# HGRN2: the gated output goes into the tile of the intra-chunk weights, and the sums of output weights are spread over other heads

## The chip, the cores and the metric

One core of a Trainium2 chip runs the whole program: a two-layer backbone (layer 0: neighbourhood attention and mLSTM; layer 1: HGRN2) over 1024 latent tokens and 256 context tokens of width 1024, all in float32. The metric is the device time of one execution in microseconds; the kernel before is given by the median of three.

## The reference

Both parts of the change lie in layer 1, the HGRN2 mixer. Cut to what matters:

```python
def _gla_chunkwise(q, k, v, lf, S):          # per head, both directions
    def step(S, xs):
        b = jnp.cumsum(lfc, axis=2)
        o = einsum('bhtk,bhkv->bhtv', qc * exp(b), S)
        pair = exp(where(tri, b[:, :, :, None, :] - b[:, :, None, :, :], -inf))
        a = einsum('bhtk,bhtsk->bhts', qc, pair * kc[:, :, None, :, :])
        o = o + einsum('bhts,bhsv->bhtv', a, vc)
        S = exp(bL[:, :, 0])[..., None] * S + einsum('bhsk,bhsv->bhkv', kc * exp(bL - b), vc)
        return S, o

def merge(o, z):
    o = _rms(o, h_norm)                      # over the 128 columns of a head
    return (o * silu(z)) @ w_out             # 16 heads x 128 columns -> 1024
```

`a` are the intra-chunk weights, `o` a head's output, `z` its gate.

## The kernel before

The 16 heads of layer 1 run one after the other in the loop of `build` (L1348 on). The recurrence is worked in 8 chunks of 128 tokens. For a head h:

- `hg_intra` (L976) makes K and Q, the diagonal product in strips of 64x64 (L1006, on `gq`, masked into `gD` at L996) and then seven levels (`hg_level`, L1025): strips of K and Q on PE (L1006, on `gksel` and `gQ`), products on DVE that carry the decay one level on (L1051, L1055), a masked copy into D (L1057). New Q comes from four products (L987). After the last level ACT copies the intra-chunk weights into the tile A (`gA`, one buffer, 128 x 8 x 128; L1061, L1062).
- `hg_vz` (L921) projects v and z: a group of 24 matmuls for v of the context (copied by ACT into the tile `gEc` at L930), then four groups of 48 matmuls of 256 columns, a pair of token tiles each ("projection matmuls", `mm<-wzh` and `mm<-wzl`, L128 to L130). From each group's PSUM bank ACT copies v (L940) and a sigmoid (L942), and DVE writes z (L943, tile `gz`, one buffer). The tag `mm` has two PSUM banks.
- `hg_close` transposes K into `gkn`; `hg_ctx` (L947) makes the context's state in the tiles `gEc`, `gq` and `gknc` (sums at L969).
- `hg_scan` (L1064) runs the states backward (L1071) and the output forward: per chunk L1082 (A times v), L1083 and L1084 (Q times the states), and L1087 for the next state. Four chunks share the one PSUM bank `acc`. After the 4th and the 8th chunk: four squares with sums on ACT (L1098), two steps of the inverse root on POOL (L154, L156), o times z on DVE (L1102), and the scaling on POOL (L1103).
- `hg_proj(h + 1)` projects the next head's decays and q (weights `wh`, `wl`).
- `hg_out` (L1135) transposes the scaled product, four chunks at a time, on PE (L1140), ACT scales it into `gyt` (L1142) and POOL's queue writes it to DRAM (L1143, `yd2`).
- `wo_sums` (L1110) prepares the output stage, which multiplies sums of blocks of the output weights: one call takes a 128 x 256 piece of each of four blocks. On POOL's queue: four loads (L1116) into `gknc` and `gEc`, four subtractions (L1117), four stores (L1123). Sixteen calls are needed; heads 0 to 7 have one each, heads 8 to 11 two.
- `y_diff` (L1126) behind heads 1 to 8 makes a difference of two halves of an earlier head's y, in the same two tiles on the same queue (L1129 to L1132).

The order of the instructions on each engine is fixed when the program is built: a planner puts them in order by priority (the strips and level products are marked urgent) and by its own notion of when each could start. So work of head h + 1 (its levels and its projection of v and z) runs between the scan and the transposes of head h; I call that stretch the seam of head h + 1, and it opens with that head's diagonal strips. `gknc` and `gEc` have one buffer each and serve `hg_vz`, `hg_ctx`, `wo_sums` and `y_diff` in turn.

Behind the loop the output stage (L1363 on) multiplies y by the prepared blocks. Its first products are planned into the last head. Its later tiles (`gbc`, `woraw`, `oys`) take over memory of the head loop's pools, and their loads are issued from SP's queue (L1399 on).

Of the kernel before, what the change touches and what calls it, by code (L numbers as in the profile page):

```python
# [13 lines left out]
ALU = mybir.AluOpType  # L14
# [4 lines left out]
P = 128  # L19
# [25 lines left out]
class Prog:  # L45
# [1018 lines left out]
    def hg_scan(self, st, H, S, pool):  # L1064
        nc = self.nc
        v, z = st["v"], st["z"]
        Sf, Sb = S
        sb = {7: Sb}
        for c in range(7, 0, -1):
            u = self.ps("s", [P, P])  # L1070
            nc.tensor.matmul(u, lhsT=H["kn"][c // 4][1][:, c % 4, :], rhs=v[:, c, :], start=True, stop=True)  # L1071
            s = self.t(pool, [P, P], F32, "gS1", 10)
            nc.vector.scalar_tensor_tensor(
                out=s, in0=sb[c], scalar=H["T"][:, 1, c : c + 1], in1=u, op0=ALU.mult, op1=ALU.add
            )
            sb[c - 1] = s
        for c in range(8):
            cs = slice(c * P, (c + 1) * P)
            if c % 4 == 0:
                o4 = self.ps("acc", [P, 4, P])  # L1080
            o = o4[:, c % 4, :]
            nc.tensor.matmul(o, lhsT=H["A"][:, c, :], rhs=v[:, c, :], start=True, stop=False)  # L1082
            nc.tensor.matmul(o, lhsT=H["Q"][:, 0, cs], rhs=sb[c], start=False, stop=False)  # L1083
            nc.tensor.matmul(o, lhsT=H["Q"][:, 1, cs], rhs=Sf, start=False, stop=True)  # L1084
            if c < 7:
                u = self.ps("s", [P, P])
                nc.tensor.matmul(u, lhsT=H["kn"][c // 4][0][:, c % 4, :], rhs=v[:, c, :], start=True, stop=True)  # L1087
                s = self.t(pool, [P, P], F32, "gS0", 2)
                nc.vector.scalar_tensor_tensor(
                    out=s, in0=Sf, scalar=H["T"][:, 0, c : c + 1], in1=u, op0=ALU.mult, op1=ALU.add  # L1090
                )
                Sf = s
            if c % 4 < 3:
                continue
            ss = self.t(pool, [P, 4], F32, "gss", 2)
            jk = self.t(pool, [P, P], F32, "gjk", 1)
            for i in range(4):
                nc.scalar.activation(jk, o4[:, i, :], AF.Square, accum_out=ss[:, i : i + 1])  # L1098
            self.rsqrt(ss, ss, 1.0 / P)

            z4 = z[:, c - 3 : c + 1, :]
            nc.vector.tensor_tensor(out=z4, in0=o4, in1=z4, op=ALU.mult)  # L1102
            nc.gpsimd.tensor_tensor(out=z4, in0=z4, in1=ss.unsqueeze(2).to_broadcast([P, 4, P]), op=ALU.mult)  # L1103

    def quarters(self, pool):
        two = [self.t(pool, [P, 2 * SQ], F32, t, 1) for t in ("gknc", "gEc")]
# [39 lines left out]
    def build(self):  # L1146
        tc, nc, a = self.tc, self.nc, self.a
        dma = nc.sync.dma_start
        with ExitStack() as es:
# [22 lines left out]
            def load(name, shape, eng=nc.gpsimd):  # L1172
# [12 lines left out]
                out=self.qkn, in0=qkn[:, 0:1], scalar1=qkn[:, 1:2], scalar2=0.125, op0=ALU.mult, op1=ALU.mult  # L1185
# [14 lines left out]
            for i in range(2):  # L1200
# [6 lines left out]
                out=self.lb[:, 1, :], in0=self.lb[:, 0, :], scalar1=-1.0, scalar2=1.0, op0=ALU.mult, op1=ALU.add  # L1207
# [35 lines left out]
            with tc.tile_pool(name="na", bufs=2) as pool, self.pp.phase(tq=1, s=2, acc=1):  # L1243
                qk = self.na_qk(0, pool)
                z = self.na_z(0, pool)
                ahead = [("k", 0), ("q", 1), ("k", 1), ("q", 2), ("k", 2), ("q", 3)]
                for p2 in range(8):
                    self.na_attn(p2, qk, z, pool)
                    if p2 < 7:
# [5 lines left out]
                        z = self.na_z(p2 + 1, pool)  # L1255
# [5 lines left out]
            with tc.tile_pool(name="ml", bufs=2) as pool, self.pp.phase(s=2, acc=2):  # L1261
# [9 lines left out]
                st, parts = self.ml_load(0, pool)  # L1271
                for ld in parts:
                    ld()
                for h in range(4):
                    nxt, parts = self.ml_load(h + 1, pool) if h < 3 else (None, None)
                    self.ml_rec(h, st, pool, parts)
                    st = nxt
# [65 lines left out]
            with l1:  # L1343
                pool = l1.enter_context(tc.tile_pool(name="hg", bufs=2))
                self.rawp = pool
                l1.enter_context(self.pp.phase(s=3, acc=1))
                st = self.hg_proj(0, pool, wf)
                for h in range(16):  # L1348
                    hv = self.hg_intra(st, pool)
                    self.hg_vz(h, st, pool)  # L1350
                    self.hg_close(hv, pool)
                    S = self.hg_ctx(st, pool)
                    self.hg_scan(st, hv, S, pool)
                    z = st["z"]
                    if h < 15:
                        st = self.hg_proj(h + 1, pool)
                    self.hg_out(h, z, pool, self.yd2)
                    for i in ([h] if h < 8 else [2 * h - 8, 2 * h - 7] if h < 12 else []):
                        self.wo_sums(i // 2, i % 2, pool)
                    if 0 < h < 9:  # L1360
                        self.y_diff(h - 1, pool)

                rh.close()  # L1363
                yp = es.enter_context(tc.tile_pool(name="oy", bufs=1, side="right"))
                wo, wr, raw = [(yp, "wo", 8)], [(self.wp, "w", 4)], [yp, 4, "woraw"]
                assert self.slabs == 4
                S, W, y2 = self.sy, a["woc"], self.yd2
                acc = [self.t(yp, [P, 4, 512], F32, f"oacc{i}", 1) for i in range(2)]
                block = lambda src, ring, later=None, raw=raw: self.wblock(
                    None, "wo", [src], 8, 512, raw, later=later, ring=ring  # L1370
                )
                p, u = acc

                def add(out, x, y, eng=nc.vector):
                    eng.tensor_tensor(out=out, in0=x, in1=y, op=ALU.add)

                w = block(W[0:D, 0:512], wo * 8, None, [self.rawp, 3, "wraw"])
                self.out_part(w, 0, 0, y2, yp, lambda t, ps: nc.scalar.copy(acc[0][:, t, :], ps))
                w = block(self.sw[1], wr * 4 + wo * 4)
                self.out_part(w, 0, 0, S, yp, lambda t, ps: add(u[:, t, :], ps, p[:, t, :]))  # L1380
                w2 = block(W[D : 2 * D, 0:512], wo * 4 + wr * 4)

                yh, yl = [[], []], [[], []]
                for k in (0, 4):
                    for t in range(2):
                        for to, fr in zip((yh[t], yl[t]), self.out_y(t, 1, y2, yp, 4, ks=(k,))):
                            to += fr
# [225 lines left out]
```

## Time and profile before

| | us |
|---|---|
| median of 3 runs | 3467.52 (3466.03 to 3476.98) |
| the profiled execution, whole | 3470.15 |
| its span | 3468.4 |
| granted PE clock over the span | 0.992 |
| head loop, diagonal of head 0 to last transposes | 1891.5 to 3326.5 |
| behind it | 141.9 |

The profile's page gives busy time by engine: PE is TensorE's matmuls, PEld its weight loads, DVE is VectorE, ACT ScalarE, POOL GpSimd, SP the queue that issues most loads. In rows in order of time, the first column is the start within the span, the second the length in us; a bracket tells how long the engine stood idle before and what it waited for. Float32 matmuls take two passes each, so x32 strips are 16 matmuls. Steps between the starts of neighbouring matmuls tell the rate, not their lengths, since they overlap.

### The profile page before, as it was taken

Reading aid. Unit: us, or ns where it says so; the run is one execution under the profiler, and the core shown is the slowest. Engines: PE = TensorE matmul, PEld = TensorE weight load, DVE = VectorE, ACT = ScalarE, POOL = GpSimd, SP = SyncE. Lnnn points to the kernel's source line nnn. Section 1 sums busy time; section 2 is a strip of 40 time slices with the busy share of each in tenths; the row PEclk is TensorE's granted clock in tenths of the full one; section 3 lists DMA queues with packets and bytes.
Section 4 is the critical chain, followed back from the end, with each engine's and each line's share of the span. In section 5 each row is a group of like instructions: output and inputs, shape, how many; then the busy total and the mean of one; then the engine's idle time right before and its main releaser. Section 6 shows DMA issues by size and latency. Waiting matters only on the chain.

```text
span 3468.4 us, 64675 instructions
## 1 busy us (share of the span) xinstructions
PE 3386.4 (98%) x25100; PEld 2983.5 (86%) x25100; DVE 2089.2 (60%) x4824; ACT 1440.2 (42%) x3353; POOL 674.2 (19%) x1044
## 2 busy tenths in 40 slices
PE   8999999999999999999999999999999999999987
PEld 5779998889989888898878999888888899998876
DVE  4546665666655566687666555555555555555667
ACT  5445554554543444454354333333333333333432
POOL 2222221222211112221100111111111322000023
PEclk9999999999999999999999999999999999999998
DMA  5542222322223434444652111111111211110364
GB/s 205 174 133 59 78 77 77 90 80 72 81 88 96 150 115 128 132 130 144 211 168 79 50 56 56 59 59 58 56 59 57 69 62 62 44 38 26 122 204 145
DMA packets 331540, 333.59 MB, mean 96 GB/s; under 512 B 30985, under 2 KB 277961, under 8 KB 331233
## 3 DMA queue, kind: packets, MB, share of 16 engines
q1 hardware_dynamic: 291008, 222.76, 21.7%
q0 software_dynamic: 40224, 106.69, 9.1%
q8 instruction: 198, 3.24, 0.4%
q14 instruction: 110, 0.89, 0.1%
HBM read 259.40 MB, written 69.79 MB: 95 GB/s over the span
## 4 chain that ended last, share of the span: by engine, by line
PE 86%; DMA 4%; DVE 3%; issue 3%; ACT 1%; POOL 1%; SPq 0%; POOLq 0%; DVEq 0%; ACTq 0%
PE mm L128 19%; PE mm L129 19%; PE mm L130 19%; PE s L1006 4%; PE acc L783 2%; PE tr L763 2%; PE mm L843 2%; PE mm L844 2%; PE mm L845 2%; PE acc L555 2%; PE s L564 2%; PE acc L545 1%; PE acc L1082 1%; PE acc L1083 1%; PE acc L1084 1%
## 5 line engine op out<-in xcount | busy, mean ns | idle before, releaser
L130 PE MATMUL mm<-hh,wl 128*128 128x512 f32 (+1 forms) x1600 | 583.6, 365 | 0.0
L128 PE MATMUL mm<-hh,wh 128*128 128x512 f32 (+1 forms) x1600 | 583.1, 364 | 0.0
L129 PE MATMUL mm<-hl,wh 128*128 128x512 f32 (+1 forms) x1600 | 581.9, 364 | 0.0
L128 PE MATMUL mm<-wh,hh 128*128 128x256 f32 (+1 forms) x1520 | 472.5, 311 | 0.9 <-ACT ev L317 0.6
L129 PE MATMUL mm<-wl,hh 128*128 128x256 f32 (+1 forms) x1520 | 471.5, 310 | 0.0
L130 PE MATMUL mm<-wh,hl 128*128 128x256 f32 (+1 forms) x1520 | 470.7, 310 | 0.3 <-DVE hl L262 0.3
L130 PEld LDWEIGHTS mm<-hh,wl 128*128 128x128 f32 x1600 | 301.8, 189 | 43.9 <-issue 0.2
L128 PEld LDWEIGHTS mm<-hh,wh 128*128 128x128 f32 x1600 | 302.0, 189 | 42.6 <-issue 0.5
L129 PEld LDWEIGHTS mm<-hl,wh 128*128 128x128 f32 x1600 | 301.9, 189 | 41.9 <-issue 0.2
L128 PEld LDWEIGHTS mm<-wh,hh 128*128 128x128 f32 x1520 | 289.8, 191 | 14.6 <-issue 1.1
L129 PEld LDWEIGHTS mm<-wl,hh 128*128 128x128 f32 x1520 | 289.8, 191 | 14.3 <-issue 2.7
L130 PEld LDWEIGHTS mm<-wh,hl 128*128 128x128 f32 x1520 | 289.7, 191 | 13.2 <-issue 1.7
L128 PE MATMUL mm<-wzh,hh 128*128 128x256 f32 x1024 | 289.8, 283 | 0.3 <-ACT gEc L930 0.3
L130 PE MATMUL mm<-wzh,hl 128*128 128x256 f32 x1024 | 289.2, 282 | 0.0
L129 PE MATMUL mm<-wzl,hh 128*128 128x256 f32 x1024 | 289.2, 282 | 0.0
L73 DVE TENSOR_TENSOR wl<-wraw,wh 128x512 fp32r<-128x512 f32 x240 | 167.0, 701 | 161.6 <-ACT wh L72 147.2
L72 ACT CAST wh<-wraw 128x512 fp32r<-128x512 f32 x240 | 147.3, 618 | 202.0 <-PE mm L129 145.4
L1036 ACT COPY gksel<-gK 128x1024 f32<-128x1024 f32 x96 | 110.8, 1154 | 223.9 <-PE s L1006 113.7
L128 PEld LDWEIGHTS mm<-wzh,hh 128*128 128x128 f32 x1024 | 193.0, 188 | 2.4 <-ACT gEc L930 0.4
L129 PEld LDWEIGHTS mm<-wzl,hh 128*128 128x128 f32 x1024 | 192.8, 188 | 1.4
L1051 DVE TENSOR_TENSOR gQ<-gQ,gF 128x1024 f32<-128x1024 f32 x112 | 139.3, 1244 | 90.4 <-PE s L1006 89.9
L130 PEld LDWEIGHTS mm<-wzh,hl 128*128 128x128 f32 x1024 | 193.0, 188 | 0.6
(391 smaller groups left out, 7549.5 us busy)
## 6 DMA issues: line engine op xcount, KB each, us to landing
wraw<-in_wab_dram SPq DMA_DIRECT2D x112, 256.0 KB
wraw<-in_wc_dram SPq DMA_DIRECT2D x96, 256.0 KB
wraw<-yd SPq DMA_DIRECT2D x94, 256.0 KB
adar<-in_wada_dram POOLq DMA_DIRECT2D x32, 512.0 KB, 4.4
wraw<-in_wc_dram SPq DMA_DIRECT2D x128, 128.0 KB
md<-ev POOLq DMA_DIRECT2D x60, 256.0 KB, 2.7
mloz<-md SPq DMA_DIRECT2D x40, 256.0 KB
adar<-in_wada_dram SPq DMA_DIRECT2D x16, 512.0 KB
```

Source lines behind the costliest of these rows:

```text
L72: nc.scalar.copy(hi, x)
L73: nc.vector.tensor_tensor(out=lo, in0=x, in1=hi.bitcast(F32), op=ALU.subtract)
L128: mm(ps, lhsT=lh(k), rhs=rh(k), start=(start and k == 0), stop=False)
L129: mm(ps, lhsT=lh(k), rhs=rl(k), start=False, stop=False)
L130: m = mm(ps, lhsT=ll(k), rhs=rh(k), start=False, stop=(stop and k == nk - 1))
L555: nc.tensor.matmul(num, lhsT=qc[:, j, :], rhs=C[d][:, j, :], start=False, stop=(j == 1))
L564: nc.tensor.matmul(u, lhsT=st["k"][c][:, j * P : (j + 1) * P], rhs=vw, start=True, stop=True)
L763: nc.tensor.transpose(pt[:nk, i, :], pr[:, o : o + nk], self.ident)
L783: m = nc.tensor.matmul(yp[h64], lhsT=v[:, h64], rhs=pTs[hd][:nk, i, :], start=(i == turn[0]), stop=(i == turn[-1]), tile_position=(0, hd * ...
L1006: self.nc.tensor.matmul(out[s], lhsT=lhsT, rhs=rhs, start=True, stop=True, tile_position=(0, b * 64))
L1036: nc.scalar.copy(ksel.rearrange("p (b s i) -> p b s i", s=2, i=h), pick(K))
L1051: nc.vector.tensor_tensor(out=v, in0=v, in1=tot, op=ALU.mult)
```

## The change

The product of output and z is written into the four chunks of A in place of z, and so is the scaled product; `hg_out` transposes A. The calls of `wo_sums` become one each for heads 0 to 11 and two each for heads 12 and 13.

```diff
-            z4 = z[:, c - 3 : c + 1, :]
-            nc.vector.tensor_tensor(out=z4, in0=o4, in1=z4, op=ALU.mult)
-            nc.gpsimd.tensor_tensor(out=z4, in0=z4, in1=ss.unsqueeze(2).to_broadcast([P, 4, P]), op=ALU.mult)
+            y4 = H["A"][:, c - 3 : c + 1, :]
+            nc.vector.tensor_tensor(out=y4, in0=o4, in1=z[:, c - 3 : c + 1, :], op=ALU.mult)
+            nc.gpsimd.tensor_tensor(out=y4, in0=y4, in1=ss.unsqueeze(2).to_broadcast([P, 4, P]), op=ALU.mult)
...
-                    z = st["z"]
                     if h < 15:
                         st = self.hg_proj(h + 1, pool)
-                    self.hg_out(h, z, pool, self.yd2)
-                    for i in ([h] if h < 8 else [2 * h - 8, 2 * h - 7] if h < 12 else []):
+                    self.hg_out(h, hv["A"], pool, self.yd2)
+                    for i in [h] if h < 12 else [2 * h - 12, 2 * h - 11] if h < 14 else []:
                         self.wo_sums(i // 2, i % 2, pool)
```

## The prediction

> **What bounds the kernel now.** I read the busy shares first, then the busy time of each engine by stage, then the order of time of PE, DVE and POOL at the seam between two heads, and last the chain of waits behind the loop.
>
> ```profile
> PE 3386.4 (98%) x25100; PEld 2983.5 (86%) x25100; DVE 2089.2 (60%) x4824; ACT 1440.2 (42%) x3353; POOL 674.2 (19%) x1044
> ```
>
> PE is the bound, and the change neither adds nor removes a matmul. So only the time in which PE stands still can be won or lost; all that follows is a count of PE's pauses. The stages of the head loop (first column the stretch, second its length, third PE's busy time):
>
> ```profile
> core 0: us, PE busy (x) PEld busy (x) DVE busy (x) ACT busy (x) POOL busy (x), PEclk, DMA share, GB/s
> 2155.60:2242.80 87.20, 86.40 (x773) 78.22 (x774) 49.77 (x82) 28.95 (x61) 14.91 (x24) 1.00 0.18 58
> 2242.80:2686.60 443.80, 434.37 (x3885) 393.52 (x3884) 246.94 (x405) 143.50 (x303) 83.80 (x122) 1.00 0.18 57
> 2686.60:2782.20 95.60, 86.19 (x761) 78.04 (x760) 56.64 (x91) 31.48 (x71) 33.77 (x47) 0.98 0.22 71
> 2782.20:3045.00 262.80, 262.80 (x2353) 239.47 (x2353) 146.85 (x235) 85.78 (x174) 46.46 (x69) 1.00 0.17 52
> 3045.00:3136.10 91.10, 90.48 (x810) 82.50 (x811) 49.42 (x82) 29.82 (x63) 6.29 (x9) 1.00 0.12 36
> 3136.10:3221.50 85.40, 83.05 (x745) 75.00 (x746) 46.68 (x78) 26.55 (x55) 6.12 (x9) 1.00 0.08 26
> ```
>
> Each row runs from one head's diagonal product (L996) to a later head's. Length less busy time is the pause: 0.80 for head 3, 9.43 for heads 4 to 8 (1.89 each), 9.41 for head 9, none for heads 10 to 12, 0.62 for head 13, 2.35 for head 14. Before head 3 there is none.
>
> The seam of heads 5 and 6, on PE and then on DVE and POOL (start, length, line, what it waited for in brackets):
>
> ```profile
> 2426.79 0.39 PE L1084 MATMUL acc<-gS,gQ 128*128 128x128 f32 x2
> 2427.14 0.28 PE L128 MATMUL mm<-wzh,hh 128*128 128x256 f32 x1
> 2427.25 0.28 PE L129 MATMUL mm<-wzl,hh 128*128 128x256 f32 x1
> 2429.86 1.56 PE L1006 MATMUL s<-gQ,gksel 128*64 128x64 f32 x32 [1.15 <-DVE gQ L987]
> 2431.86 0.66 PE L1140 MATMUL tr<-ident,gz 128*128 128x128 f32 x4 [0.43 <-POOL gz L1103]
> 2433.03 1.18 PE L1006 MATMUL s<-gQ,gksel 128*64 128x64 f32 x32 [0.30 <-DVE gQ L1051]
> ```
>
> ```profile
> 2427.22 2.50 DVE L987 TENSOR_TENSOR gQ<-gq,gF 128x512 f32<-128x512 f32 x4 [2.58 <-PE acc L1084]
> 2431.46 1.43 DVE L1051 TENSOR_TENSOR gQ<-gQ,gF 128x1024 f32<-128x1024 f32 x1 [0.81 <-PE s L1006]
> 2433.43 0.41 DVE L943 TENSOR_TENSOR gz<-gsg,mm 128x256 f32<-128x256 f32 x1
> 2430.76 1.04 POOL L1103 TENSOR_TENSOR gz<-gz,gss 128x512 f32<-128x512 f32 x1
> 3233.74 1.18 PE L1006 MATMUL s<-gQ,gksel 128*64 128x64 f32 x32 [0.62 <-DVE gQ L1051]
> ```
>
> The last scan matmul ends, DVE makes the new Q (four L987), and only then may the level-0 strips run. PE has 13 projection matmuls of 0.12 (the step from 2427.14 to 2427.25) to fill that, and then nothing: strips, transposes of z, strips follow each other with a wait each, 1.15 + 0.43 + 0.30 = 1.88. The reason is the third row: L943, the first write of the next head's z, runs right after the transposes at 2431.86, since z has one buffer and they read it. Until then the PSUM bank that L943 empties is held, and of two banks the other is full too, so no further projection group can start. The last row is the same wait at head 15's seam.
>
> Head 9's seam is worse. Head 8 has two sums of output weights and the difference of y in POOL's queue:
>
> ```profile
> 2687.74 0.49 PE L1082 MATMUL acc<-gv,gA 128*128 128x128 f32 x2 [1.12 <-DVE gz L1102]
> 2692.38 0.66 PE L1140 MATMUL tr<-ident,gz 128*128 128x128 f32 x4 [1.70 <-POOL gz L1103]
> 2694.23 1.56 PE L1006 MATMUL s<-gQ,gksel 128*64 128x64 f32 x32 [1.19 <-DVE gQ L987]
> 2697.20 1.18 PE L1006 MATMUL s<-gQ,gksel 128*64 128x64 f32 x32 [1.41 <-DVE gQ L1051]
> 2702.96 1.98 PE L1006 MATMUL s<-gQ,gksel 128*64 128x64 f32 x32 [3.99 <-DVE gQ L1051]
> 2687.05 0.19 POOL L154 TENSOR_SCALAR gss<-gss 128x4 f32<-128x4 f32 x1 [2.75 <-ACT gjk L1098]
> 2687.32 0.72 POOL L1117 TENSOR_TENSOR gEc<-gEc,gknc 128x256 f32<-128x256 f32 x1
> 2690.91 1.42 POOL L1103 TENSOR_TENSOR gz<-gz,gss 128x512 f32<-128x512 f32 x1
> 2699.61 2.12 POOL L1131 TENSOR_TENSOR gknc<-gknc,gEc 128x512 f32<-128x512 f32 x1 [1.43 <-DMA gEc<-yd]
> 2690.72 3.37 DVE L987 TENSOR_TENSOR gQ<-gq,gF 128x512 f32<-128x512 f32 x4 [0.99 <-PE acc L1084]
> 2700.52 2.29 DVE L1051 TENSOR_TENSOR gQ<-gQ,gF 128x1024 f32<-128x1024 f32 x1
> ```
>
> Here not one projection matmul stands between the diagonal strips and the level-2 strips. The five waits make 9.41, and the last strips take 1.98 in place of 1.18, 0.8 more.
>
> **The change part by part.** The product o·z (32 x L1102) and the scaling on POOL (32 x L1103) keep size and count; they write A in place of z, and the 128 transposes read A. Same engines, same 128x512: nothing in itself. A's own readers (L1082) of those four chunks are over when o4 is complete, so L1102 gains only a wait for the L1103 of a whole head earlier: nothing. A's next writers (L1061, L1062) come at the end of the next head's levels, tens of microseconds behind the transposes: nothing, covered by six levels.
>
> What moves is z's release: from the transposes to L1102, which in DVE's queue stands just ahead. In the changed kernel's instruction order L943 comes directly behind L957, ahead of the level-0 products, and PE's order between the last scan matmul and the level-1 strips, for heads 4 to 12, goes from "13 projection matmuls, strips, 4 + 2 transposes, strips" to "18, strips, 21, 4 + 2 transposes, 4, strips". Now each wait in turn. Q: five more matmuls of 0.12 take 0.6 off 1.15, 0.55 is left. The transposes: 21 x 0.12 = 2.5 more cover against 0.43, none left. Level 1: four more, none left. L943 (0.41) must end before the third group starts; behind L957 it ends about as the strips do, and I add 0.1. Per seam 0.65 is left; its bounds are 0 and 1.25 (the Q wait kept whole). Heads 4 to 8: 9.43 − 5 x 0.65 = 6.2 won. Head 3 (38 matmuls ahead of its strips in the new order): 0.8 won. Heads 10 to 12 take the same new order and lose what they did not have: 3 x 0.65 = 1.95 lost. Head 14 (44 matmuls ahead of its strips) wins 2.35, head 15 (26 matmuls between its strips) the 0.6 of the row at 3233.74.
>
> The sums: 16 stay 16, each with four loads, four subtractions and four stores on POOL's queue. Head 8 loses its second sum, so head 9's seam has the new order like the rest: 9.41 − 0.65 = 8.8 won, and the 0.8 of slow strips. Heads 9 to 11 lose one each; their two sums cost no pause now, so nothing. Heads 12 and 13 get two. Behind head 13 the order keeps 54 projection matmuls between diagonal and level-0 strips, and the sums stand ahead of L154 in POOL's queue: nothing. Behind head 12 the order again has no projection between the diagonal strips and the level-0 strips, and the last subtraction and two stores stand between L154 and L1103. I take the rows of head 9: 1.12 for the bank, 1.70 less one subtraction (0.72) for the transposes, 1.19 for Q, and 0.4 for the rest, since 7 and 11 matmuls follow and there is no y difference (no 3.99): 3.7 against 0.62 now, 3.1 lost. Bounds: 0, as behind heads 9 to 11 now, and 9.41 + 0.8, as in head 9.
>
> By the Trainium skill ("SBUF — State Buffer", section "SBUF: two separate sides") a DVE operation with two SBUF inputs and a POOL operation that reads SBUF exclude each other for a whole instruction. The stretched rows (L987 3.37 for 2.50, L1051 2.29 for 1.23 beside L1131) agree. By that rule two subtractions and L1103 could each hold an L987 behind head 12, an estimate of 2.5 in place of the 0.87 seen, 1.6 less won in all: 3452.0 in place of the sum below.
>
> Behind the loop:
>
> ```profile
> 3326.54 0.66 PE L1140 MATMUL tr<-ident,gz 128*128 128x128 f32 x4 [4.53 <-POOL gz L1103]
> 3329.30 0.80 PE L128 MATMUL mm<-wh,yh 128*128 128x512 f32 x1 [2.10 <-ACT yh L72]
> 3303.22 0.24 PE mm L843
> 3329.89 0.63 PE L129 MATMUL mm<-wl,yh 128*128 128x512 f32 x1
> 3330.32 0.63 PE L130 MATMUL mm<-wh,yl 128*128 128x512 f32 x1
> 3330.14 3.64 DMA yd<-gyt
> 3334.28 5.81 DMA gbc<-gated
> 3340.15 5.90 DMA woraw<-sw
> ```
>
> Now the last head's second transposes come right behind its scan and wait 4.53, then PE waits 2.10 for y; ten matmuls run at a step of 0.43 (the last two PE rows) for 0.24. In the new order 32 output matmuls stand between. PE could win 4.5 + 2.1 + 2.0 = 8.6. But what follows hangs on the chain in the last three rows: y written, the gate loaded into memory that the head loop gives back, then weights. In the new order the second transposes stand 8 matmuls later in the sum of work (8 x 0.24 = 1.9) and have no wait of 4.53: 2.6 earlier. Their copy on ACT stands behind four casts of y in place of one; the first half's transposes come some 40 matmuls ahead of the second, so these casts find their data, and I let them cost nothing. I take 2.6, as the transfers decide; the other end is 5.9 lost, if the changed order of SP's loads puts one weight load (5.90) late.
>
> The sum: 6.2 + 0.8 + 8.8 + 0.8 + 2.35 + 0.6 − 1.95 − 3.1 + 2.6 = 17.1 won. The profiled execution takes 3470.15, 2.6 over the median of 3467.52; off the median this makes 3450.4.
>
> **The rivals.** First, the waits only change places: Q's whole wait stays in all nine seams (0.6 x 9 = 5.4) and head 12's seam costs what head 9's does now (10.2 for 3.7, 6.5 more). For it: the new order behind head 12 looks like head 9's. Against it: no y difference there. Then 17.1 − 11.9 = 5.2 is won, 3462.3. Second, PE and not the transfers sets the end: 8.6 in place of 2.6, 3444.4. For it: PE pauses often there; against it: 5.81 and 5.90 in a row on the chain. Third, the slower side, one mechanism in heads 1 to 8:
>
> ```profile
> 2595.60 1.27 POOL L1131 TENSOR_TENSOR gknc<-gknc,gEc 128x512 f32<-128x512 f32 x1 [2.66 <-DMA gEc<-yd]
> 2596.91 0.37 ACT L930 COPY gEc<-mm 128x256 f32<-128x256 f32 x1
> ```
>
> ACT's copy of v (L930) needs gEc, which POOL holds until L1131 ends (2596.87, copy at 2596.91). In the new order L930 stands ahead of L940, L942 and the four squares, so if POOL's sum and difference end late, the squares, L1102, the bank and PE all wait behind it. Now 25 matmuls and the strips cover that path and no bank wait is seen in heads 4 to 8; in the new order it is 20, so I put the slack at about 1, from which on it decides. Were two landings late by the length of one (2.66 each), a seam would cost 5.3 − 1 = 4.3, eight of them 34: 3467.5 − 17.1 + 34 = 3484.8. Against it: those landings repeat in every head within tenths, and in the new order some 3 us more of matmuls stand between the context's sums, which start POOL's work, and the seam. Fourth, the earlier release does nothing, since something else holds the banks, and head 9's seam alone becomes like its neighbours (9.41 − 1.89 + 0.8 = 8.3, less 3.1): 5.2 won, 3462.3.
>
> **How the numbers follow.** Forecast 0.55, waits change places 0.14, PE sets the end 0.15, slower 0.08, release does nothing 0.08. About 0.3%, 10.4 us, is what a measurement of this kernel can tell from no change, so faster means under 3457.1. The forecast, which I would trust to 7 either way, and the second rival lie there but for the forecast's upper end; the first and fourth lie within 0.3%. Faster 0.71, same 0.21, slower 0.08. The range takes in the cases at 3462 and the lower one with a margin for bounds that add: 3438 to 3464.
>
> **What would show it.** Right: in heads 4 to 12 L943 ahead of the second transposes; those transposes and the level-1 strips without a wait; some half a microsecond left on L987; head 9's seam like its neighbours; a pause of 2 to 5 behind head 12; no 4.53 behind the loop, and the gate's load 2 to 3 us earlier against the end of the scan. Wrong: pauses on the bank (L1082 after L1102) in every head would be the third rival, a stall of 9 behind head 12 the first, and a loop shortened by 14.5 with a longer output stage would mean that the changed load order took it back.

## The result, and the profile after

The changed kernel takes 3447.01 us (median of 4 runs, 3445.79 to 3449.74) against 3470.16 for the kernel before beside it on the same chip (4 runs): a ratio of 0.9932, 95% interval 0.9914 to 0.9951. In a second set of runs it took 3449.60 against 3469.44 (0.9938, 0.9926 to 0.9951). The forecast was 3450.4. Its profiled execution takes 3449.74 with a span of 3448.0, 20.4 less than the span of 3468.4 before.

The stages of the changed kernel in the same cut as before (stretch, length, PE's busy time, ...; the last two rows are the stretch from head 15's diagonal to the issue of the gate's load, L1398, and from there to the end):

```profile
2154.10:2243.20 89.10, 89.10 (x799) 81.37 (x800) 49.62 (x82) 29.39 (x61) 16.47 (x25) 1.00 0.18 57
2243.20:2681.00 437.80, 434.99 (x3891) 396.01 (x3891) 248.38 (x405) 147.68 (x305) 81.92 (x121) 1.00 0.18 58
2681.00:2768.70 87.70, 87.14 (x780) 79.35 (x780) 50.07 (x81) 29.48 (x61) 14.08 (x21) 1.00 0.16 49
2768.70:3030.40 261.70, 258.61 (x2313) 235.11 (x2313) 150.33 (x244) 88.15 (x182) 44.97 (x69) 1.00 0.17 52
3030.40:3115.00 84.60, 82.09 (x734) 74.22 (x735) 50.72 (x83) 28.90 (x60) 25.50 (x37) 1.00 0.21 66
3115.00:3203.50 88.50, 88.50 (x795) 80.82 (x796) 46.90 (x78) 26.92 (x57) 5.86 (x8) 1.00 0.08 25
3203.50:3310.90 107.40, 103.99 (x783) 90.28 (x783) 68.58 (x113) 49.38 (x103) 10.04 (x14) 0.97 0.42 131
3310.90:3448.00 137.10, 110.61 (x433) 86.06 (x432) 101.95 (x125) 42.05 (x73) 51.27 (x44) 0.90 0.63 196
```

The last two stretches of the kernel before, cut at its own gate load, and that load's issue on SP's queue:

```profile
3221.50:3333.90 112.40, 99.67 (x746) 85.44 (x747) 67.39 (x112) 48.56 (x101) 9.98 (x14) 0.95 0.38 121
3333.90:3468.40 134.50, 111.68 (x447) 87.32 (x445) 103.03 (x127) 43.06 (x74) 53.73 (x44) 0.91 0.64 202
```

```profile
3333.89 0.81 SPq L1399 DMA_DIRECT2D gbc<-gated  x2
```

Length less busy time is PE's pause in each stretch. Beside it what the prediction's terms come to:

| PE's pauses, us | before | forecast | after |
|---|---|---|---|
| head 3 | 0.80 | 0 | 0 |
| heads 4 to 8 | 9.43 | 3.2 | 2.81 |
| head 9 | 9.41 | 0.65 | 0.56 |
| heads 10 to 13 | 0.62 | 5.65 | 5.60 |
| head 14 | 2.35 | 0 | 0 |
| head 15 to the gate's load | 12.73 | | 3.41 |
| from there to the end | 22.82 | | 26.49 |
| the last two together | 35.55 | 32.35 | 29.90 |

The pauses fall by 58.16 − 38.87 = 19.3; the other 1.1 of the 20.4 is work that runs faster (head 9's slow strips among it). In the loop nearly every row is the forecast's; behind it PE wins 9.3 ahead of the gate's load and gives 3.7 back behind it. (In a second profiled execution of the changed kernel the last two rows are 3.90 and 25.08: 8.8 won and 2.3 given back.)

The seam of heads 5 and 6 in the changed kernel, PE and then DVE in order of time:

```profile
2425.44 1.56 PE L1006 MATMUL s<-gQ,gksel 128*64 128x64 f32 x32 [0.56 <-DVE gQ L987]
2429.45 0.60 PE L1140 MATMUL tr<-ident,gA 128*128 128x128 f32 x4
2422.80 2.50 DVE L987 TENSOR_TENSOR gQ<-gq,gF 128x512 f32<-128x512 f32 x4 [2.59 <-PE acc L1084]
2425.21 0.68 DVE L1102 TENSOR_TENSOR gA<-acc,gz 128x512 f32<-128x512 f32 x1
2426.15 0.41 DVE L943 TENSOR_TENSOR gz<-gsg,mm 128x256 f32<-128x256 f32 x1
```

L943, the first write of the next z, starts at 2426.15, 0.9 behind the start of the product and 3.3 ahead of the transposes; it stood behind them before. The bank is free, projection groups fill PE's queue, and of the three waits (1.15, 0.43, 0.30) only 0.56 on L987 is left; the stage's 2.81 is five times that.

The seam of head 13, behind the first head with two sums (PE, DVE, POOL):

```profile
3030.53 0.49 PE L1082 MATMUL acc<-gv,gA 128*128 128x128 f32 x2 [1.19 <-DVE gA L1102]
3034.05 0.65 PE L1140 MATMUL tr<-ident,gA 128*128 128x128 f32 x4 [0.58 <-POOL gA L1103]
3036.51 1.56 PE L1006 MATMUL s<-gQ,gksel 128*64 128x64 f32 x32 [1.80 <-DVE gQ L987]
3033.51 2.85 DVE L987 TENSOR_TENSOR gQ<-gq,gF 128x512 f32<-128x512 f32 x4 [0.99 <-PE acc L1084]
3030.05 0.73 POOL L1117 TENSOR_TENSOR gEc<-gEc 128x256 f32<-128x256 f32 x1
3032.95 1.05 POOL L1103 TENSOR_TENSOR gA<-gA,gss 128x512 f32<-128x512 f32 x1
```

Three waits, 3.57 in all, in the places that the forecast took from head 9's old seam: bank, transposes, Q. No projection stands between the diagonal strips and the level-0 strips there.

Behind the loop (the last scan matmuls and the second transposes on PE, then ACT, DVE and PE behind the gate's load):

```profile
3298.32 0.39 PE L1084 MATMUL acc<-gS,gQ 128*128 128x128 f32 x2
3306.76 0.60 PE L1140 MATMUL tr<-ident,gA 128*128 128x128 f32 x4
3321.36 1.33 ACT L72 CAST woh<-woraw 128x512 fp32r<-128x512 f32 x2 [7.82 <-DMA woraw<-sw]
3325.66 0.62 ACT L72 CAST yh<-oys 128x512 fp32r<-128x512 f32 x1 [2.96 <-DVE oys L1425]
3323.83 2.35 DVE L1425 TENSOR_TENSOR oys<-oys,oyz 128x512 f32<-128x512 f32 x2
3326.33 0.80 PE L843 MATMUL mm<-woh,yh 128*128 128x512 f32 x1 [3.41 <-ACT yh L72]
```

The transposes no longer wait (4.53 before): output matmuls fill the 8 us between them and the scan. But 15 us later PE stands 3.41: ACT's cast of the weights waited 7.82 for their load, DVE's two sums of y (L1425) stand in its queue behind work on those weights (L73), and the cast of y waits for them.

### The profile page after: what moved, and what is told of

Read it like the earlier page. It is cut to its first block, busy times and chain, and to the rows that moved or that the text cites. A ratio compares the mean times of both kernels' runs of the same rounds, so it can differ in the third digit from the quotient of the medians.

```text
span 3448.0 us, 64658 instructions
## 1 busy us (share of the span) xinstructions
PE 3388.6 (98%) x25100; PEld 2988.2 (87%) x25100; DVE 2089.0 (61%) x4824; ACT 1443.8 (42%) x3353; POOL 669.7 (19%) x1044
## 4 chain that ended last, share of the span: by engine, by line
PE 91%; DVE 3%; DMA 2%; issue 1%; ACT 1%; POOL 0%; SPq 0%; POOLq 0%; DVEq 0%; ACTq 0%
PE mm L130 20%; PE mm L128 20%; PE mm L129 20%; PE s L1006 4%; PE acc L783 3%; PE tr L763 2%; PE mm L843 2%; PE mm L845 2%; PE mm L844 2%; PE acc L555 2%; PE s L564 2%; PE acc L545 1%; PE acc L1082 1%; PE acc L1083 1%; PE acc L1084 1%
## 5 line engine op out<-in xcount | busy, mean ns | idle before, releaser
L73 DVE TENSOR_TENSOR wl<-wraw,wh 128x512 fp32r<-128x512 f32 x240 | 168.5, 708 | 119.4 <-ACT wh L72 113.0
L72 ACT CAST wh<-wraw 128x512 fp32r<-128x512 f32 x240 | 147.2, 619 | 211.9 <-PE mm L129 156.1
L843 PE MATMUL mm<-woh,yh 128*128 128x512 f32 x422 | 171.9, 407 | 14.8 <-ACT yh L72 8.3
```

The lines of the kernel that those rows point to most:

```text
L72: nc.scalar.copy(hi, x)
L73: nc.vector.tensor_tensor(out=lo, in0=x, in1=hi.bitcast(F32), op=ALU.subtract)
L843: mm(ps, lhsT=yh[k], rhs=w.h(kk), start=(kk == 0), stop=False)
```

## The experiments

Each variant was timed four or five times with the kernel before beside it (medians of 3469.93, 3469.92 and 3469.44). The stretch ahead of head 0's diagonal, in which no kernel differs, ended between 1889.1 and 1896.3 in the profiled executions, so a single span can be 3.5 off by that alone; times are compared by medians, causes by the pauses (length less busy time) of three stretches: the loop from head 0's diagonal to head 15's, from there to the gate's load, and from the gate's load to the end (10.8 of which lie behind the last matmul). The pauses are those of one execution each; the two executions of the changed kernel differ by 0.02, 0.49 and 1.41 in the three columns.

| run | median, us | ratio to before (95%) | loop | to gate's load | to the end |
|---|---|---|---|---|---|
| before | 3470 | 1 | 22.61 | 12.73 | 22.82 |
| changed | 3447.01 | 0.9932 (0.9914 to 0.9951) | 8.97 | 3.41 | 26.49 |
| product into A alone | 3454.72 | 0.9956 (0.9942 to 0.9969) | 8.81 | 10.09 | 23.77 |
| sums moved alone | 3458.21 | 0.9967 (0.9954 to 0.9979) | 23.89 | 3.29 | 21.50 |
| product into v's tile | 3450.70 | 0.9943 (0.9931 to 0.9956) | 9.01 | 3.18 | 26.44 |
| pairs in heads 0, 1 | 3450.12 | 0.9942 (0.9929 to 0.9954) | 6.74 | 10.82 | 21.96 |
| pair in head 13 | 3439.77 | 0.9914 (0.9901 to 0.9928) | 9.64 | 2.86 | 19.53 |
| pair in head 14 | 3442.33 | 0.9923 (0.9910 to 0.9935) | 7.78 | 6.78 | 21.79 |
| pairs in heads 0 to 7 | 3457.73 | 0.9964 (0.9951 to 0.9976) | 10.02 | 9.83 | 20.84 |
| no loads of x at the end | 3438.61 | 0.9915 (0.9901 to 0.9928) | 8.97 | 3.84 | 19.50 |
| one sum in every head | 3447.99 | 0.9938 (0.9924 to 0.9952) | 6.75 | 6.84 | 24.10 |
| changed, once more | 3449.60 | 0.9938 (0.9926 to 0.9951) | 8.95 | 3.90 | 25.08 |

**The product into A, without moving the sums.**

```diff
-                    for i in [h] if h < 12 else [2 * h - 12, 2 * h - 11] if h < 14 else []:
+                    for i in ([h] if h < 8 else [2 * h - 8, 2 * h - 7] if h < 12 else []):
```

> The product goes into A, the sums stay as before (one for heads 0 to 7, two for heads 8 to 11). Theory (z's release opens PE's covers in every seam, the sums only choose which seam is left uncovered): heads 4 to 8 pause 0.56 each as in the changed kernel, head 3 none; head 9's seam, which again has two sums and the difference of y and no projection matmul between the diagonal strips and the level-2 strips, keeps some 3.5 to 5 of its 10.2 (the changed kernel's head 13 pays 3.51 for the same pattern); heads 10 to 14 pause under 0.5 each. Sum against before: 7.4 + 5.5 + 3.0 + 0.6 and 2 to 5 behind the loop, 18 to 21 won: level with the changed kernel within 3 us. Rival (the two edits add up, each with its own share, as the sum of the prediction has it: 6.5 of the 17 belong to the moved sums): head 9's seam stays at 9 to 10 and only 11 to 14 are won, 6 to 9 us slower than the changed kernel.

Measured: 15.2 faster than before by the medians, 5 to 8 slower than the changed kernel (3449.60 and 3447.01). Its waits at head 9's seam, PE in order of time:

```profile
2680.33 0.49 PE L1082 MATMUL acc<-gv,gA 128*128 128x128 f32 x2 [1.19 <-DVE gA L1102]
2686.85 1.98 PE L1006 MATMUL s<-gQ,gksel 128*64 128x64 f32 x32 [3.58 <-DVE gQ L987]
```

The two sums and the difference of y are all there, and still 9.41 of waits became 4.77: z's release alone took about half. The loop is as the theory has it (8.81 of pauses, as good as the changed kernel's 8.97), so the rival's seam of 9 to 10 fell. But the total lies between both: behind the loop only 1.7 of pauses went, less than the 2 to 5 expected, and the second transposes wait there as before:

```profile
3312.64 1.12 PE L1140 MATMUL tr<-ident,gA 128*128 128x128 f32 x4 [4.23 <-POOL gA L1103]
```

**The sums moved, without the product into A.**

Against the kernel before:

```diff
-                    for i in ([h] if h < 8 else [2 * h - 8, 2 * h - 7] if h < 12 else []):
+                    for i in [h] if h < 12 else [2 * h - 12, 2 * h - 11] if h < 14 else []:
```

> The sums move (one for heads 0 to 11, two for 12 and 13), the product stays in z. Theory: heads 4 to 8 keep 1.89 each, head 9 falls from 10.2 to 1.9 (8.3 won), heads 10 to 12 rise from 0 to 1.9 each (5.7 lost), head 13's seam takes head 9's pattern without the difference of y (3 to 5 lost): within 3 us of before. Rival (the two edits add up): 6 to 7 us faster than before.

Measured: 11.7 faster, which neither expected. The stage rows (head 13 to 14, and the last two stretches):

```profile
3047.50:3140.10 92.60, 87.90 (x759) 79.96 (x759) 55.60 (x90) 31.26 (x69) 28.59 (x42) 0.94 0.20 65
3224.80:3330.00 105.20, 101.91 (x780) 89.74 (x781) 67.14 (x109) 47.06 (x100) 9.51 (x12) 0.97 0.42 133
3330.00:3460.30 130.30, 108.80 (x447) 85.08 (x445) 101.76 (x127) 43.24 (x75) 55.08 (x44) 0.95 0.66 206
```

In the loop the theory held: 23.89 of pauses against 22.61, nothing won, the 4.7 of head 13 in place of head 9's. The whole gain is in the last two stretches, 24.79 of pauses against 35.55. So it is the sums' new places, not z's release, that leave work for the end of the scan: in this kernel's order 37 output matmuls stand between the last scan matmul and the second transposes, in the changed one 36 (the prediction's 32 of y's first block and 4 more), in the two kernels whose sums end at head 11 none. The two edits do not add: in the loop all is z's, behind it nearly all is the sums' (10.8 against 1.7), and behind the gate's load both together are worse (26.49) than either alone (23.77, 21.50).

**The product into v's tile.**

```diff
-            y4 = H["A"][:, c - 3 : c + 1, :]
+            y4 = v[:, c - 3 : c + 1, :]
...
+                    y = st["v"]
                     if h < 15:
                         st = self.hg_proj(h + 1, pool)
-                    self.hg_out(h, hv["A"], pool, self.yd2)
+                    self.hg_out(h, y, pool, self.yd2)
```

> The changed kernel, but the product goes into v's tile (two buffers, its chunks dead at that point) instead of A's. Theory (what counts is that z is released at the product; the tile that takes it is free of waits): PE's pauses as in the changed kernel, 0.56 in each of heads 4 to 12, time level within 2 us. Rival (A itself costs something: L1102 or L1103 waits for A's readers or writers and half a microsecond per seam comes from that): the pauses of 0.56 go, 4 to 5 us faster.

Measured: pauses equal to the changed kernel's to 0.3 in each stretch, time 1 to 4 above it, within what the runs scatter. The same seam, first on PE, then on DVE:

```profile
2425.97 1.56 PE L1006 MATMUL s<-gQ,gksel 128*64 128x64 f32 x32 [0.56 <-DVE gQ L987]
2426.67 0.41 DVE L943 TENSOR_TENSOR gz<-gsg,mm 128x256 f32<-128x256 f32 x1
```

The 0.56 is no price of A. Another tile that is dead at that point does as well; what counts is that z is let go at the product.

**The pairs of sums in heads 0 and 1.**

```diff
-                    for i in [h] if h < 12 else [2 * h - 12, 2 * h - 11] if h < 14 else []:
+                    for i in [2 * h, 2 * h + 1] if h < 2 else [h + 2] if h < 14 else []:
```

> The changed kernel with the doubled sums in heads 0 and 1 and one sum for heads 2 to 13, so that the doubling does not start in the middle of the loop. Theory (the seam behind the first doubled head loses its cover, because the longer POOL queue delays z's scaled product against the projections): head 13's 3.51 becomes 0.6, head 14's seam 0.6 in place of 0, heads 1 to 3 stay without a pause; in the loop 2 to 3 us won; behind the loop the last head's second transposes stand right behind its scan again and wait 4 to 5, which costs 0 to 3: level with the changed kernel or 2 us faster. Rival (two sums in one head cost POOL's time wherever they stand): heads 1 and 2 pause 3 to 4 each, 3 to 6 us slower than the changed kernel.

Measured: level with the changed kernel (3450.12 against 3447.0 to 3449.6). Heads 1 to 3 do not pause, head 13 pauses 0.68, head 14 0.67: the loop wins 2.2, as the theory has it. Behind the loop the last transposes stand right behind the scan and wait 4.23 again, as in the first variant; PE loses 7.4 ahead of the gate's load and wins 4.5 behind it. Sums up to head 13 are thus not enough to leave output matmuls for that wait: they were left where the doubling stood late (heads 12 to 14, 36 or 37) or a sum in head 15 (33). Why the planner orders them so was not tried further.

**The pair one head later.**

```diff
-                    for i in [h] if h < 12 else [2 * h - 12, 2 * h - 11] if h < 14 else []:
+                    for i in [h] if h < 13 else [2 * h - 13, 2 * h - 12] if h < 14 else [15] if h < 15 else []:
```

> The changed kernel with one sum for heads 0 to 12, two for head 13 and one for head 14: the doubling starts one head later. Theory (the seam behind the first doubled head pays, and by what the runs so far show the same doubling leaves output matmuls for the end of the scan: 36 of them there in the changed kernel, whose pauses ahead of the gate's load are 3.4 us against 10.1 to 12.7 where none stands there): head 13's seam falls from 2.4 to 0.7 without its bank wait, head 14's rises from 0 to 2.4 to 3.5, heads 4 to 12 stay at 0.56 and 0.68; 37 output matmuls stand between the last scan matmul and the second transposes, no wait of 4 there, last stretch (head 15's diagonal to the end) between the 24.8 of the sums alone and the 29.9 of the changed kernel: 0 to 5 us faster than the changed kernel. Rival (the pauses of the last stretch depend on z's release and not on the sums): last stretch 30 or more, nothing won.

Measured: 3439.77, 7 to 10 faster than the changed kernel and 30 faster than before; the fastest kernel of the study that computes everything. Head 14's seam, then the last two stretches:

```profile
3116.98 0.49 PE L1082 MATMUL acc<-gv,gA 128*128 128x128 f32 x2 [1.19 <-DVE gA L1102]
3120.51 0.66 PE L1140 MATMUL tr<-ident,gA 128*128 128x128 f32 x4 [0.58 <-POOL gA L1103]
3122.96 1.84 PE L1006 MATMUL s<-gQ,gksel 128*64 128x64 f32 x32 [1.80 <-DVE gQ L987]
```

```profile
3202.40:3306.30 103.90, 101.04 (x786) 89.01 (x787) 67.77 (x111) 47.29 (x100) 10.75 (x14) 0.98 0.43 135
3306.30:3436.50 130.20, 110.67 (x449) 86.65 (x447) 101.58 (x127) 43.37 (x75) 54.81 (x44) 0.94 0.67 206
```

The pattern of three waits (1.19, 0.58, 1.80, the same to the hundredth) has moved with the doubling from head 13's seam to head 14's, so it belongs to the seam behind the head where the sums go from one to two. The last two stretches have 22.4 of pauses, less than the 24.8 to 29.9 expected, and the gain is above the 0 to 5; over the changed kernel it is all behind the gate's load (19.53 against 26.49). There SP's order of issue differs, first this kernel, then the changed one:

```profile
3306.29 0.81 SPq L1398 DMA_DIRECT2D gbc<-gated  x2
3307.15 0.90 SPq L1405 DMA_DIRECT2D oxh<-x  x2
3308.15 0.85 SPq L101 DMA_DIRECT2D woraw<-sw  x2
...
3313.92 1.30 ACT L72 CAST woh<-woraw 128x512 fp32r<-128x512 f32 x2 [3.53 <-DMA woraw<-sw]
```

```profile
3310.87 0.81 SPq L1398 DMA_DIRECT2D gbc<-gated  x2
3311.72 1.39 SPq L1405 DMA_DIRECT2D oxh<-x  x3
3313.16 0.43 SPq L1416 DMA_DIRECT2D oys<-yd  x1
3313.69 1.22 SPq L101 DMA_DIRECT2D woraw<-sw  x2
```

In the changed kernel the first weights stand behind three loads of x and one of y, and ACT's cast starts on them 10.5 behind the gate's load (3321.36 − 3310.87) in place of 7.6 (3313.92 − 3306.29). That this order makes the difference is not shown: with one sum in every head (below) the loads start in this kernel's order, the cast comes 7.8 behind the gate's load (3325.80 − 3318.03), and PE still pauses 24.10.

**The pair in head 14.**

```diff
-                    for i in [h] if h < 12 else [2 * h - 12, 2 * h - 11] if h < 14 else []:
+                    for i in [h] if h < 14 else [14, 15] if h < 15 else []:
```

> The changed kernel with one sum for heads 0 to 13 and two for head 14. Theory: heads 13 and 14 pause 0.7 each, the uncovered seam is head 15's (3 to 4 us, in the last stretch), 36 output matmuls stand behind the last scan matmul, no wait of 4 there: loop 6.7, last stretch 29 to 34, level with the changed kernel within 3 us. Rival (the doubled sums cost more the later they stand, since the output stage waits for the stores of the blocks that they make): last stretch 38 or more, 5 us slower or worse.

Measured: 3442.33, 5 to 7 faster than the changed kernel, where level was expected. The loop has 7.78 of pauses where 6.7 was expected: heads 13 and 14 pause about 0.7, and the bank wait of 1.19 stands ahead of head 15's diagonal. The uncovered seam is head 15's with 1.68 and 1.19, the last two stretches have 28.6 of pauses, a little under the 29 expected. The rival, that late sums delay the output stage, fell.

**Pairs in all of heads 0 to 7.**

```diff
-                    for i in [h] if h < 12 else [2 * h - 12, 2 * h - 11] if h < 14 else []:
+                    for i in [2 * h, 2 * h + 1] if h < 8 else []:
```

> Two sums for each of heads 0 to 7 and none later, product into A. PE's order is the one of the run with doubled heads 0 and 1; POOL's queue and its transfers alone are fuller in heads 2 to 7, with the difference of y behind the two sums. The prediction's third rival in its own terms: ACT's copy of v (L930) waits for POOL's difference (L1131), slack about 1 us, from which on every seam of heads 3 to 8 pays. Theory: L1131 and L930 come some 8 us later in each of these heads, but still ahead of the second four squares, so the seams stay at 0.56 to 1 each: level with the run of doubled heads 0 and 1 within 3 us. Rival: 1 to 4 us in each of the seams of heads 3 to 8, 6 to 24 us slower.

Measured: 7.6 slower than with pairs in heads 0 and 1, the rival's lower end. Against the expectation PE's order was not the same: its stretches from diagonal to diagonal hold 742 to 811 matmuls in heads 3 to 9, where a steady one has 779. In three of them (heads 3, 6 and 8) PE pauses 2.2 to 2.3, in the other four not at all. Head 8's looks like the prediction's third rival (POOL, ACT and PE there; the last row is ACT in head 3's seam):

```profile
2600.31 1.28 POOL L1131 TENSOR_TENSOR gknc<-gknc,gEc 128x512 f32<-128x512 f32 x1 [0.95 <-DMA gEc<-yd]
2603.01 0.69 ACT L1142 ACTIVATE gyt<-tr,hnc 128x512 f32<-128x512 f32 x1
2603.60 0.36 ACT L930 COPY gEc<-mm 128x256 f32<-128x256 f32 x1
2604.01 0.58 PE L128 MATMUL mm<-wzh,hh 128*128 128x256 f32 x1 [2.23 <-ACT gEc L930]
2165.31 0.37 ACT L930 COPY gEc<-mm 128x256 f32<-128x256 f32 x1 [2.47 <-POOL gknc L1131]
```

A projection group waits 2.23 for ACT's copy L930. But the difference of y is over at 2601.59, 2.0 ahead of that copy; the copy stands directly behind ACT's four squares and the scaling of y (L1142), so PE waits here for ACT's order and not for POOL. In head 3's seam ACT does wait 2.47 for the difference, and PE does not wait for that copy: its pause there is 2.24 on the new Q. So the rival's path is not seen whole even with an extra sum per head. The three pauses cost 3.3 of the loop (10.02 against 6.74). Another 2.8 is the same 11712 matmuls of the loop at work for longer (1311.78 against 1308.96): the granted clock was 0.50 for 3.4 us right behind the pauses of heads 3 and 8 (from 2163.6 and 2603.9), and nowhere in the loop of the run with pairs in heads 0 and 1. The spans are 7.9 apart, and 2.3 of that lies ahead of head 0, where the kernels do not differ.

**Without the loads of x behind the loop.**

```diff
-                    dma(out=xt, in_=self.x1[r, c])
...
-                    add(xt, xt, g, eng)
+                    add(xt, g, g, eng)
```

> The changed kernel without the 16 loads of the residual x behind the loop (L1405; the last sum adds the gated product to itself instead of to x), 4 MB less to load behind the gate's load; PE, DVE and POOL do the same work. Theory (behind the gate's load the transfers set PE's pauses: the DMA share is 0.91 and 1.11 in the first 30 us there): the pauses behind the gate's load fall from 15.7 to 8 to 12, 4 to 8 us faster than the changed kernel. Rival (DVE's and PE's own work sets the end there; DVE is busy 15.00 of 15 us between 60 and 90 us behind the gate's load): under 2 us faster.

Measured: 3438.61, 8 to 11 faster than the changed kernel, more than the 4 to 8 expected; loop and the stretch to the gate's load unchanged, 7.0 less of pauses behind the gate's load, 19.50 with the 10.8 behind the last matmul, so 8.7 where 8 to 12 was expected. The row of that stretch:

```profile
3311.70:3436.80 125.10, 105.60 (x433) 82.63 (x432) 99.16 (x125) 41.16 (x73) 57.99 (x44) 0.94 0.59 181
```

PE does the same 433 matmuls as in the changed kernel; 10 to 12 us of the stretch (135.2 and 137.1 in two executions of it) went with 4 MB of loads. Of these, 5.6 to 7.0 are pauses; the rest is the same matmuls at work for 105.60 in place of 110.12 and 110.61, at a granted clock of 0.94 in place of 0.91 and 0.90. Transfers set a good part of the pauses there. Order of issue and amount of traffic are not told apart by this run.

**One sum in every head.**

```diff
-                    for i in [h] if h < 12 else [2 * h - 12, 2 * h - 11] if h < 14 else []:
+                    for i in [h]:
```

> The changed kernel with one sum for every head, 0 to 15, so that no head has two and the last sum stands in head 15. Theory (a seam pays where the doubling begins; output matmuls are left for the end of the scan where the last sums stand late): all seams of heads 4 to 14 pause 0.56 to 0.7, 7 in all in the loop; 33 output matmuls stand between the last scan matmul and the second transposes, no wait of 4 there; last stretch 24 to 30: 3438 to 3443, level with or up to 3 us faster than the kernel with the pair in head 13. Rival (the output stage waits for the stores of the last blocks, and the later the sums stand the more it costs): pauses of 3 or more on weights (L843 to L845 behind woraw) in head 15 or behind the gate's load, 3446 or more.

Measured: 3447.99, level with the changed kernel; the 3438 to 3443 was missed. The loop is as the theory has it (6.75, no seam above 0.7: without a head that doubles no seam is uncovered). Behind it PE waits in many places; a long one behind the gate's load:

```profile
3332.93 0.70 PE L843 MATMUL mm<-woh,yh 128*128 128x512 f32 x1 [2.85 <-ACT yh L72]
```

This wait is on y (L72), not on a block that the last sum stored: its chain goes back over DVE's sum of y (L1425) to a load of y (`oyz`), landed 7.45 behind its issue. Of all waits of PE from head 15's diagonal to the end, 0.5 is on weights (`woh`). So the rival's number came in, but not its cause; what makes the end of this kernel longer than expected stays open.

**The changed kernel once more.**

> The changed kernel once more, beside the last variant on the same chip. Both theories: 3447 to 3451, its pauses 9.0 in the loop and about 30 in the last stretch, again with a half-clock stretch of 6.8 us around head 15's level products and near the first blocks behind the gate's load.

Measured: 3449.60; 8.95 of pauses in the loop and 28.98 in the last two stretches, 6.8 us of half clock at 3239.4 and 3348.6.

## Why the prediction was right, point by point

- **PE's pauses are all there is to win.** Right: 19.3 of 20.4.
- **z's release, heads 3 to 8.** Right in place and size: L943 ahead of the transposes, 0.56 left where 0.65 was taken. That A itself costs nothing is shown by the run with v's tile.
- **Head 9's seam, 8.8 + 0.8.** The size is right (9.41 to 0.56), the reason is half of it. The prediction put it down to head 8's lost second sum. The first two runs show that each edit alone does a large part: with both sums left and z released 4.77 remains, with the sum gone and z kept 1.89.
- **Heads 10 to 12, 1.95 lost.** Right: 2.03 (5.60 − 3.57). It is the moved sums that take this: with two sums there and the product in A the heads pause 0.
- **Head 12's two sums, 3.7 at head 13's seam.** Right: 3.57, as 1.19 + 0.58 + 1.80 where 1.12 + 0.98 + 1.19 + 0.4 was summed. The runs add the rule behind it: the uncovered seam is the one behind the head where the count goes from one to two (the seams of heads 9, 13, 14 and 15 in the runs); that it is the planner's order that does this was not tried apart.
- **Heads 14 and 15.** Right: both waits gone.
- **By the Trainium skill's exclusion of POOL and DVE** ("SBUF — State Buffer", section "SBUF: two separate sides") 1.6 was to be lost behind head 12. It was not: the last subtraction was over at 3030.78, ahead of L987's start at 3033.51, and beside L1103 (0.49 of overlap) L987 took 2.85 for 2.50, so 0.35 was lost.
- **Behind the loop, 2.6.** Half of the mechanism is right (output matmuls fill the wait), and its size is the one term that was off: with the 0.6 of head 15 the forecast has 3.2, and 5.65 was measured. PE's own gain ahead of the gate's load was 9.32, close to the 8.6 + 0.6 of the second rival; "I take 2.6, as the transfers decide" left out that the transfers can hand part of it on. What was lost again behind the gate's load is 3.67 (2.3 in the second execution), within the other bound of that term (5.9). That transfers set a good part of these pauses is shown by the run without the loads of x; that the loss is "one weight load late" is not. ACT's cast of the first weights does start later behind the gate's load than before (10.5 against 3342.40 − 3333.89 = 8.5), but without the loads of x it starts as late (3322.17 − 3311.69 = 10.5) and the stretch pauses least (19.50), and with one sum in every head it starts at 7.8 and the stretch pauses 24.10. Which load's place costs the 3.67 stays open.
- **The sum.** 17.1 was forecast, and the spans differ by 20.4; most of the difference is the term behind the loop. That this term is off by no more than 2.4 is partly luck: it came about as 9.3 won less 3.7 lost, and neither is a part of the forecast's 2.6. The moved sums brought that gain (10.8 behind the loop, against 1.7 for z's release alone), which the prediction did not say.
- **"The gate's load 2 to 3 us earlier against the end of the scan."** Wrong as put: it is issued 12.2 behind the scan's last matmul (3310.87 against 3298.71) where it was 11.9 (3333.89 against 3322.01), since the matmuls that fill the wait stand in that stretch. It is earlier in the program, by 23.0 against the 20.4 of the whole.
- **Rivals.** Waits that change places: no, Q's wait shrank. Release does nothing: no. The slower side: no. In the changed kernel L930 does stand ahead of the squares and wait for POOL's difference (head 8: ACT idle for 10.84, copy at 2588.06), but behind it ACT idles another 0.92 until PE's next group is there, about the slack of 1 that the prediction gave it; the run with pairs in heads 0 to 7 did not show the path whole either. PE sets the end: true up to the gate's load, not behind it.

## What to carry to other kernels

When one engine is 98% busy, count its pauses by stage and ask of each which buffer's release would let the next work be queued: here a dead tile as the target of one product let go of a single-buffered tile ahead of the transposes instead of behind them and was worth 13.8 us of pauses in the loop, with no instruction added. In the loop, side work on an off-path queue was best spread evenly, since the seam behind the head where it went from one sum to two lost its cover each time; but moving it can pay or cost at a quite different place (here the end, 10.8 us), so run each half of a two-part change alone before giving it a share of the gain. A wait won ahead of a stage that transfers fill is not yet time won: of 9.3 won ahead of the gate's load 3.7 were lost again behind it.

## What the runs showed of the hardware

The same pauses can cost different amounts. Head 13's seam pauses 1.19, 0.58 and 1.80 (to 0.01) in both executions of the changed kernel; the 3.4 us behind it, first in the first, then in the second execution (the last three figures are granted clock, DMA share, GB/s):

```profile
3038.00:3041.40 3.40, 3.40 (x40) 3.27 (x40) 3.21 (x6) 1.66 (x2) 1.02 (x2) 1.00 0.20 77
```

```profile
3038.00:3041.40 3.40, 3.40 (x24) 3.28 (x20) 2.92 (x3) 1.33 (x2) 1.33 (x2) 0.50 0.22 82
```

40 matmuls at full clock in the one, 24 at half clock in the other, and that head takes 86.0 from diagonal to diagonal in place of 84.6. By the clock records of the traces the stretches of half clock start, in each trace, on one grid of 3.413 us. In the first execution a window of that grid runs from 3034.98 to 3038.39 and holds 1.53 of the pause of 1.80; in the second one runs from 3034.62 to 3038.03 and holds all of it, and half clock follows. The Trainium skill ("TensorE: Matmul & The Clock Gate", section "Part 1: The HAM clock gate (the "warmup" mystery)") has a free-running window of about 3.4 us, which would make it a matter of how the pauses fall into it; the two executions agree. Its "after ≥1 idle window" does not: in the kernel with the sums moved alone PE worked for 1.56 of a window of 3.4 us, and half clock followed:

```profile
2787.40:2790.80 3.40, 1.56 (x32) 1.40 (x32) 2.59 (x6) 1.01 (x6) 2.73 (x4) 0.99 0.22 82
2790.80:2794.20 3.40, 3.06 (x36) 2.73 (x38) 3.40 (x7) 2.16 (x4) 0.91 (x2) 0.50 0.00 0
```

In all twelve traces, from 1880 to 3430 us, each of the 60 windows at full clock in which PE paused 1.75 us or more was followed by half clock, none in which it paused 1.56 or less, and one of the seven between. So about half a window of pauses is enough here (an estimate from these counts), and pauses of some 2 us can cost more than their length. Head 9's strips of 1.98 in the kernel before stand in such a stretch: its wait of 3.99 fills a whole window, and the clock was 0.50 from 2702.5 for 3.4 us.
